# Fifteen more entries in the table that reorders a hybrid attention layer's instruction queues

## The chip, the cores and the metric

The kernel runs on one core of one Trainium2 chip. The metric is the device time of one execution in microseconds (us); "the time" of a kernel is the median of its runs. The core has five engines that this text speaks of: TensorE (PE), VectorE (DVE), ScalarE (ACT), GpSimd (POOL) and SyncE (SP). Each works through its own queue of instructions in order. Here SP does no arithmetic: it issues the kernel's DMA transfers.

## The reference

The program is one layer of a streaming encoder. It takes 1024 prompt rows and 32 sample rows of width 1024, and projects them, after a norm, with one matrix `w_in` to q, k, v and a gate g for two groups of eight heads of 64: group A is band attention (a frame sees its own chunk of 64 and the eight before, with a clipped relative bias), group B is stick-breaking attention. The 32 sample rows also attend to cached keys and values.

```python
def band_attention(q, k, v, q_pos, k_pos, bias_table):
    s = jnp.einsum('bqhd,bkhd->bhqk', q, k).astype(jnp.float32) * ATTN_SCALE
    ...
    w = jax.nn.softmax(s, axis=-1).astype(v.dtype)
    return jnp.einsum('bhqk,bkhd->bqhd', w, v)
def stick_breaking(q, k, v, q_pos, k_pos):
    ...
    after = lax.cumsum(log_1m, axis=3, reverse=True) - log_1m
    w = jnp.where(causal, jnp.exp(log_beta + after), 0.0).astype(v.dtype)
    return jnp.einsum('bhqk,bkhd->bqhd', w, v)
def finish(h, oa, ga, ob, gb, w_out, g_post, p, w_ple, w_ple_gate):
    y = jnp.concatenate([oa * jax.nn.silu(ga), ob * jax.nn.silu(gb)], axis=-1) @ w_out
    h = h + rmsnorm(y, g_post)
    return h + jax.nn.sigmoid(h @ w_ple_gate) * (p @ w_ple)
```

The outputs are both groups of rows and the new k and v of both head groups. All is float32.

## The kernel before

Each float32 operand of a matrix product is split into a high part, a rounded copy, and a low part, the difference (`hnh` and `hnl` for the normed rows, `wh` and `wl` for weights, `kd` and `kl` for keys, `wTh` and `wTl` for attention weights). A product is three matmuls on such parts. ACT mostly casts the high parts; DVE or POOL subtract for the low ones.

The work runs over head pairs 0 to 3 of each group. For a pair of heads the columns of q, k, v are projected (`mm_qA`, `mm_kB` and so on, 352 rows at a time), k and v are turned and stored to the outputs, and then each of the two heads is attended to in eight tiles of 128 rows: scores (`SA`, `SB`), the weights (ACT's exponentials with DVE's minima for A, sigmoids and DVE's scans for B), turned weights, and values (`PVA`, `PVB`). The gates' projections (`mm_gA`, `mm_gB`) come late, then the output projection and what follows it. While attention goes on, the projections of the next pair fill PE's time. The names in the profile count pairs and heads: `swapA31_7` belongs to group A, pair 3, head 1.

Most weights are turned on PE, by `ptwA` and `ptwB`. Tiles 5, 6 and 7 of a group A head, and 4, 5, 6 of group B, take a tour through memory instead (`weights_t`, L1114): DVE turns squares of 32, one DMA stores them in a scratch (`swapA`, 960 KB for A's three tiles), four DMAs load them in another order into `wTl` (240 KB each), ACT casts them to `wTh`, and POOL subtracts in `wTl`. Then PE's `PVA` matmuls can read both.

Two other users of the queue of transfers matter here. The gate matrix and the output matrix get a preparation of their own: quarters `gB` and `oB` of 256 KB are loaded, POOL combines them, and `sum_drg` and `sum_dro` store the results. And the raw columns of `w_in` come as `wr` tiles of 256 KB, two for each projection, which ACT casts.

At the start PE runs twelve `idle` matmuls on zeros, then turns p (`pp`, two parts of 256 KB, to `ptp`), spreads the row `grow` of `g_pre` over all partitions with ones (`gpre`; DVE first casts the row into `wTl` and subtracts), and multiplies p with `w_ple` (`ple`). DVE's norm of x reads `gpre`.

No engine's order is written out by hand. `Recorder` records every operation. `order` (L499) plans from costs and sets the order on each engine. Then `moved` (L576) corrects it by the table `MOVES` (L130): an entry `(engine, i, d)` takes instruction i out of that engine's list and puts it back d places on, or back if d is negative. Entries apply one after the other, so each index counts in the list that those before it have left. Last, `emit` (L616) writes all in the merged order, and the framework adds the semaphore waits. As every operation is written from one line, the profile shows L626 for nearly all of them.

All of SP's transfers go to one DMA queue. Each is given one of eight semaphores in turn, so besides its data an issue waits for the landing of the transfer eight places before it. Whatever is moved in SP's list therefore shifts both the transfers and these waits.

Of the kernel before, what the change touches and what calls it, by code (L numbers as in the profile page):

```python
# [125 lines left out]
def f(ap):  # L126
# [12 lines left out]
    ("DVE", 228, -1), ("ACT", 822, 1), ("SP", 518, 4), ("SP", 532, 9), ("SP", 91, 1),  # L139
    ("SP", 204, 4), ("SP", 115, 10), ("DVE", 492, 7), ("PE", 2963, -10), ("PE", 2964, -10),  # L140
    ("PE", 2965, -10), ("PE", 2966, -10), ("PE", 2967, -10), ("PE", 2968, -10), ("PE", 2969, -10),
    ("PE", 2970, -10), ("PE", 2971, -10),
)


# [1986 lines left out]
```

## Time and profile before

| | |
|---|---|
| time, median of 3 runs | 767.8 us (767.15 to 769.6) |
| the profiled execution's own time | 767.8 us |
| its span, first to last instruction | 766.0 us |
| mean granted TensorE clock | 0.999 |
| busy PE, DVE, ACT, POOL | 757.5, 571.1, 542.2, 509.2 us |
| the one queue of transfers | 164.44 MB, 73.4% of 16 DMA engines' span |

The busy rows are sums over one execution. The chain of waits says which engine ended last at each moment; the waits list says for what an engine stood still, and the timeline shows single instructions with their start, length and the idle time ahead of them. A wait is named by the last of the semaphores to come. SPq in a row is SP's queue issuing a transfer, not the transfer itself.

### The profile page before, as it was taken

To read this page: it belongs to the slowest core of one execution; us is meant where nothing else is said; L and a number is where in the kernel's file an instruction comes from. 1 tells how busy PE (TensorE), PEld (TensorE's weight loads), DVE (VectorE), ACT (ScalarE), POOL (GpSimd) and SP (SyncE) were. 2 spreads that over 40 slices of the span, in tenths; PEclk is the share of its full clock that TensorE was granted. 3 is DMA by queue.
4 is the path that set the end of the run, shared out by engine and by line. 5 is a ranking of instruction groups with operands and counts; after the bars stand their busy time and mean duration, and the time that the engine had idled before them with its cause. 6 is when DMAs were issued, how large, how long until landed. Compare 5 with 4: busy or idle time off the path is not lost.

```text
span 766.0 us, 14225 instructions
## 1 busy us (share of the span) xinstructions
PE 757.5 (99%) x4502; PEld 705.8 (92%) x4502; DVE 571.1 (75%) x1029; ACT 542.2 (71%) x1139; POOL 509.2 (66%) x547
## 2 busy tenths in 40 slices
PE   8999999999999999999999999999999999999997
PEld 7999999999999999999999998999998877888786
DVE  6827567688788778878797577879455787998975
ACT  5647977788688768898897677555438868766461
POOL 5724778996637657669994747788552539697533
PEclk9999999999999999999999999999999999999999
DMA  9646977759776657986859788879578967769644
GB/s 299 219 131 188 243 220 205 219 157 266 183 186 182 148 146 230 214 248 174 212 172 264 173 234 206 240 213 268 167 255 278 319 212 223 260 203 374 218 145 138
DMA packets 198397, 165.35 MB, mean 216 GB/s; under 512 B 65889, under 2 KB 165385, under 8 KB 198322
## 3 DMA queue, kind: packets, MB, share of 16 engines
q1 hardware_dynamic: 198322, 164.44, 73.4%
q8 instruction: 36, 0.59, 0.3%
q14 instruction: 39, 0.32, 0.2%
HBM read 105.72 MB, written 58.91 MB: 215 GB/s over the span
## 4 chain that ended last, share of the span: by engine, by line
PE 92%; ACT 3%; DMA 3%; SPq 1%; DVE 1%; issue 0%; POOL 0%; ACTq 0%; DVEq 0%
PE mm_qA L626 6%; PE mm_kA L626 6%; PE mm_vA L626 6%; PE mm_gB L626 6%; PE mm_gA L626 5%; PE mm_qB L626 5%; PE mm_kB L626 5%; PE mm_vB L626 5%; PE PVB L626 4%; PE SB L626 4%; PE PVA L626 4%; PE SA L626 3%; PE ple L626 3%; PE g1P L626 3%; PE o3P L626 3%; PE o1P L626 3%
## 5 line engine op out<-in xcount | busy, mean ns | idle before, releaser
L626 POOL TENSOR_TENSOR be<-be,om 128x1024 f32<-128x1024 f32 (+8 forms) x66 | 81.8, 1246 | 43.2 <-DVE om L626 13.2
L626 DVE TENSOR_TENSOR_SCAN om<-om,SB 128x384 f32<-128x384 f32 (+5 forms) x96 | 91.6, 965 | 19.3 <-ACT om L626 13.5
L626 POOL TENSOR_TENSOR wTl<-wTl,wTh 128x640 fp32r<-128x640 f32 (+2 forms) x42 | 72.6, 1746 | 15.0 <-ACT wTh L626 11.7
L626 ACT ACTIVATE om<-SB 128x384 f32<-128x384 f32 (+5 forms) x96 | 44.2, 494 | 12.5 <-DVE SB L626 8.4
L626 ACT ACTIVATE be<-SB 128x512 f32<-128x512 f32 (+5 forms) x96 | 45.5, 495 | 9.8 <-PE SB L626 7.4
L626 ACT ACTIVATE be<-be,statA 128x640 f32<-128x640 f32 (+3 forms) x64 | 44.4, 695 | 9.0 <-DVE statA L626 8.8
L626 DVE STREAM_TRANSPOSE om<-be 128x640 f32<-128x640 f32 (+2 forms) x48 | 42.9, 899 | 2.6 <-POOL be L626 1.4
L626 ACT CAST wTh<-wTl 128x640 fp32r<-128x640 f32 (+2 forms) x48 | 35.9, 778 | 11.3 <-DMA wTl<-swapA 7.8
L626 POOL TENSOR_TENSOR oB<-oB,oB 128x256 f32<-128x256 f32 x32 | 26.8, 857 | 13.4 <-DMA oB<-in_w_out_dram 13.4
L626 DVE CUSTOM_DVE_ANT_0 be<-SA,biasA 128x320 f32<-128x320 f32 (+3 forms) x64 | 30.2, 482 | 4.9 <-PE SA L626 3.8
L626 PE MATMUL SB<-kl,LB 128*128 128x384 f32 (+5 forms) x96 | 32.5, 345 | 0.0
L626 PE MATMUL SB<-kdB,LB 128*128 128x384 f32 (+5 forms) x96 | 32.3, 341 | 0.0
L626 POOL TENSOR_TENSOR kl<-stkB,kdB 64x1024 fp32r<-64x1024 f32 x8 | 19.7, 2460 | 18.7 <-ACT kdB L626 17.3
L626 DVE TENSOR_TENSOR wTl<-ptwB,wTh 128x512 fp32r<-128x512 f32 (+3 forms) x48 | 26.1, 547 | 5.7 <-ACT wTh L626 5.1
L626 PE MATMUL SA<-kl,LA 128*128 128x320 f32 (+2 forms) x96 | 30.1, 316 | 0.0
L626 DVE TENSOR_TENSOR SB<-SB,maskb 128x128 f32<-128x128 f32 x64 | 18.0, 293 | 16.0 <-PE SB L626 15.0
L626 PE MATMUL SA<-kdA,LA 128*128 128x320 f32 (+2 forms) x96 | 29.9, 313 | 0.0
L626 ACT CAST wTh<-ptwB 128x512 fp32r<-128x512 f32 (+3 forms) x48 | 22.8, 482 | 9.9 <-PE ptwB L626 9.3
L626 DVE TENSOR_TENSOR wTl<-ptwA,wTh 128x512 fp32r<-128x512 f32 (+3 forms) x48 | 22.5, 480 | 8.9 <-ACT wTh L626 8.1
L626 PE MATMUL PVB<-wTl,v2B 128*128 128x256 f32 (+1 forms) x144 | 24.8, 295 | 0.0
L626 POOL TENSOR_TENSOR gB<-gB,gB 128x256 f32<-128x256 f32 x32 | 24.6, 790 | 0.1
L626 POOL TENSOR_TENSOR h<-h,x 128x512 f32<-128x512 f32 (+1 forms) x18 | 23.8, 1344 | 0.2 <-DVE h L626 0.2
(700 smaller groups left out, 2667.1 us busy)
## 6 DMA issues: line engine op xcount, KB each, us to landing
swapA<-om SPq DMA_DIRECT2D x8, 960.0 KB, 5.7
wTl<-swapA SPq DMA_DIRECT2D x32, 240.0 KB, 5.1
oB<-in_w_out_dram SPq DMA_DIRECT2D x16, 256.0 KB, 3.6
sum_dro<-oB SPq DMA_DIRECT2D x16, 256.0 KB, 4.0
gB<-in_w_ple_gate_dram SPq DMA_DIRECT2D x16, 256.0 KB, 4.3
sum_drg<-gB SPq DMA_DIRECT2D x16, 256.0 KB, 2.5
x<-in_x_prompt_dram SPq DMA_DIRECT2D x16, 256.0 KB, 4.2
h_dr<-h SPq DMA_DIRECT2D x8, 512.0 KB, 3.8
```

Source lines behind the costliest of these rows:

```text
L626: getattr(getattr(tc.nc, o.what[0]), o.what[1])(*args, **kw)
```

## The change

Fifteen entries are added at the end of `MOVES`; nothing else differs. As the table grows by three lines, L626 becomes L629.

```diff
-    ("PE", 2970, -10), ("PE", 2971, -10),
+    ("PE", 2970, -10), ("PE", 2971, -10), ("SP", 2, -1), ("SP", 486, -2), ("SP", 493, -2),
+    ("SP", 494, -2), ("SP", 495, -2), ("SP", 496, -2), ("SP", 197, 6), ("SP", 486, -2),
+    ("SP", 92, -1), ("SP", 330, 4), ("SP", 509, -2), ("SP", 198, 1), ("DVE", 237, -4),
+    ("SP", 445, 6), ("POOL", 335, -1),
```

Thirteen entries are for SP, one is for DVE and one for POOL. They are listed below in the order of the program; one of SP's, (92, -1), exchanges two transfers that read alike. PE's and ACT's orders stay.

1. At the start, p's second part goes ahead of the row of `g_pre`.

SP at the start of the program, before:

```order
L626 DMA pp0_176<-in_p_prompt_dram 128x2x256
L626 DMA grow_171<-in_g_pre_dram 1x1024
L626 DMA pp0_176<-in_p_prompt_dram 128x2x256
L626 DMA wpr0_0True_177<-in_w_ple_dram 128x512
L626 DMA om_179<-in_x_prompt_dram 128x1024
```

And after:

```order
L629 DMA pp0_176<-in_p_prompt_dram 128x2x256 x2
L629 DMA grow_171<-in_g_pre_dram 1x1024
L629 DMA wpr0_0True_177<-in_w_ple_dram 128x512
L629 DMA om_179<-in_x_prompt_dram 128x1024
L629 DMA wpr1_0True_178<-in_w_ple_dram 128x512
```

Both parts of p now stand together, and the row of one partition behind them.

2. In the tour of head 0 of pair 1 (`swapA10_7`), the store of `vtA1` to the output of new A values goes behind six other transfers: the third and fourth load of the tour, a quarter of the output matrix, a load from `cache_a_v` and two stores of new keys.

SP between the first two loads of this tour and the cache load `be`, before (`oB213` is a quarter of the output matrix, `o_dr4` takes a finished piece of head group B, `out_4` is the output of new B keys):

```order
L626 DMA wTl_170<-swapA10_7_123 32x12x160 x2
L626 DMA o_dr4_67<-otB01_0_0_2137 64x256
L626 DMA o_dr4_67<-otB01_0_1_2288 64x256
L626 DMA out_3_dram<-vtA1_1981 128x4x128
L626 DMA wTl_170<-swapA10_7_123 32x12x160
L626 DMA oB213_2557<-in_w_out_dram 128x512
L626 DMA wTl_170<-swapA10_7_123 32x12x160
L626 DMA be_193<-in_cache_a_v_dram 128x4x256
L626 DMA out_4_dram<-ktB1_2441 32x32x32 x2
```

And after:

```order
L629 DMA wTl_170<-swapA10_7_123 32x12x160 x2
L629 DMA o_dr4_67<-otB01_0_0_2137 64x256
L629 DMA o_dr4_67<-otB01_0_1_2288 64x256
L629 DMA wTl_170<-swapA10_7_123 32x12x160 x2
L629 DMA oB213_2557<-in_w_out_dram 128x512
L629 DMA be_193<-in_cache_a_v_dram 128x4x256
L629 DMA out_4_dram<-ktB1_2441 32x32x32 x2
L629 DMA out_3_dram<-vtA1_1981 128x4x128
```

The third and fourth load now stand together, ahead of `oB213`, and the store stands behind all of them.

3. In pair 2's tour of head 0 (`swapA20_7`), the four loads of `wTl` go ahead of a store `sum_drg`. In pair 3's tour of head 0 (`swapA30_7`), the first of the four loads goes behind the stores `swapA3`, `vs_dr` and two of `o_dr`.

4. In the last A tour (`swapA31_7`), the store goes ahead of one load of a `wr_gA` tile, and the four loads go ahead of another and of a `sum_drg` store.

SP around this tour, before (`one_dr3` takes sums of the softmax, `o_dr3` finished pieces of head group A):

```order
L626 DMA wr_gA1_0_5877<-in_w_in_dram 128x4x128
L626 DMA wr_gA1_1_5878<-in_w_in_dram 128x4x128
L626 DMA swapA31_7_144<-om_179 128x1920
L626 DMA o_dr3_66<-otA30_0_0_5887 64x256
L626 DMA o_dr3_66<-otA30_0_1_5888 64x256
L626 DMA wr_gA2_0_5990<-in_w_in_dram 128x4x128
L626 DMA one_dr3_74<-sumA30_3168 16x32
L626 DMA wr_gA2_1_6005<-in_w_in_dram 128x4x128
L626 DMA sum_drg_86<-gB213_5882 128x512
L626 DMA wTl_170<-swapA31_7_144 32x12x160 x4
```

And after:

```order
L629 DMA wr_gA1_1_5878<-in_w_in_dram 128x4x128
L629 DMA swapA31_7_144<-om_179 128x1920
L629 DMA wr_gA1_0_5877<-in_w_in_dram 128x4x128
L629 DMA o_dr3_66<-otA30_0_0_5887 64x256
L629 DMA o_dr3_66<-otA30_0_1_5888 64x256
L629 DMA wr_gA2_0_5990<-in_w_in_dram 128x4x128
L629 DMA one_dr3_74<-sumA30_3168 16x32
L629 DMA wTl_170<-swapA31_7_144 32x12x160 x4
L629 DMA wr_gA2_1_6005<-in_w_in_dram 128x4x128
L629 DMA sum_drg_86<-gB213_5882 128x512
```

The store stands one place earlier and the four loads two; `wr_gA1_0` now follows the store, `wr_gA2_1` and `sum_drg` follow the loads.

5. A load from `cache_b_k` goes ahead of the store of `swapB30_6`. On DVE, the first of two minima of tile 4 of head 1 of pair 1 (`SA11_4`) goes up ahead of four subtractions and sums; on POOL, the subtraction for `wl_vB3_0` goes up ahead of a half of a `gB223` subtraction.

## The prediction, made before the changed kernel ran

> **What bounds the kernel now.** I read the page first: its busy shares, then the chain that ended last, then the waits of TensorE (PE), and then the timeline at each of these waits.
>
> ```profile
> span 766.0 us, 14225 instructions
> PE 757.5 (99%) x4502; PEld 705.8 (92%) x4502; DVE 571.1 (75%) x1029; ACT 542.2 (71%) x1139; POOL 509.2 (66%) x547
> PE 92%; ACT 3%; DMA 3%; SPq 1%; DVE 1%; issue 0%; POOL 0%; ACTq 0%; DVEq 0%
> PE idle L626 <- DVE newh L626: 1.3, 1, 1.3
> PE PVA L626 <- POOL wTl L626: 1.0, 1, 1.0
> PE ptp L626 <- DMA pp<-in_p_prompt_dram: 0.9, 1, 0.9
> PE PVA L626 <- ACT wTh L626: 0.5, 2, 0.4
> ```
>
> PE works 99% of the span, and the chain of waits runs through it for 92%. All its waits together are 1.3 + 1.0 + 0.9 + 0.5 = 3.7 us. The first, 1.3 us before the first instruction, belongs to memsets that the change leaves alone. The change removes no arithmetic and leaves PE's order and ACT's as they were, so as long as TensorE's clock stays as it is, it can win at most the other 2.4 us, a little more where a wait also empties PE's pipeline. The profiled execution took 767.8 us, 1.8 around its span of 766.0; the median is 767.8 as well (767.15 to 769.6), so sums against the one hold for the other. About 0.3%, 2.3 us, is what a measurement of this kernel can tell from no change: the bounds are 765.5 and 770.1.
>
> **The start: p's second part ahead of the row of g_pre.** In these rows a time stands first, then a length; the bracket names the idle time ahead and what ended it.
>
> ```profile
> 1.24 0.35 SPq L626 DMA_DIRECT2D grow<-in_g_pre_dram  x1
> 1.30 2.93 PE L626 MATMUL idle<-newh 128*128 128x256 f32 x12 [1.30 <-DVE newh L626]
> 1.63 0.40 SPq L626 DMA_DIRECT2D pp<-in_p_prompt_dram  x1
> 3.71 0.68 DVE L626 CAST wTl<-grow 1x1024 fp32r<-1x1024 f32 x1 [0.31 <-DMA grow<-in_g_pre_dram]
> 4.42 1.21 DVE L626 TENSOR_TENSOR wTl<-grow,wTl 1x1024 fp32r<-1x1024 f32 x1
> 6.02 1.12 PE L626 MATMUL ptp<-ident,pp 128*128 128x128 f32 x4 [0.93 <-DMA pp<-in_p_prompt_dram]
> 6.79 2.06 PE L626 MATMUL gpre<-wTl,ones 128*128 128x512 f32 x4
> 8.64 2.40 PE L626 MATMUL ple<-wph0True,php 128*128 128x512 f32 x6
> 10.88 0.86 PE L626 MATMUL ple<-wpl0True,php 128*128 128x512 f32 x3
> 11.57 1.56 PE L626 MATMUL ple<-wph1True,php 128*128 128x512 f32 x6
> ```
>
> Moved past one issue, p's second part starts 1.63 - 1.24 = 0.39 us earlier and, if its 4.3 us of flight stay, ends PE's wait by as much: at most 0.4 us is gained. The row of g_pre is issued 0.39 later. Its flight was 1.24 to 3.71, 2.5 us; if that stays, VectorE (DVE) has its CAST and subtraction (0.68 + 1.21) done at 1.63 + 2.47 + 1.92 = 6.0, and the gpre matmuls, from 6.4 on, need the second half of it only at 7.2. But the row now stands behind 256 KB. If it lands no sooner than p, at 5.6, the subtraction ends at 7.5, the third gpre matmul starts 0.3 later than it would, and nearly all is lost again; if p keeps its landing at 5.97, so that the row comes then too, 0.2 us is lost outright. So the ends are a gain of 0.4 and a loss of 0.2. I take a gain of 0.2: p surely moves, and the row's measured 2.5 us is nearer to a small transfer of its own than to p's 4.3.
>
> [...]
>
> **The second A tour of head pair 1 (190 to 205 us).** The 256 KB store of vtA goes behind the fourth wTl load and the load of a w_out quarter, oB. These rows show the loads, oB's reader and PE's reader.
>
> ```profile
> 189.78 0.54 SPq L626 DMA_DIRECT2D out_dram<-vtA  x1
> 191.67 0.59 SPq L626 DMA_DIRECT2D wTl<-swapA  x1
> 196.88 1.43 POOL L626 TENSOR_TENSOR oB<-oB,oB 128x256 f32<-128x256 f32 x2 [1.44 <-DMA oB<-in_w_out_dram]
> 198.55 1.98 ACT L626 CAST wTh<-wTl 128x640 fp32r<-128x640 f32 x3 [2.55 <-DMA wTl<-swapA]
> 199.35 5.26 POOL L626 TENSOR_TENSOR wTl<-wTl,wTh 128x640 fp32r<-128x640 f32 x3 [1.04 <-ACT wTh L626]
> 200.58 1.50 PE L626 MATMUL PVA<-wTh,v2A 128*128 128x512 f32 x8 [0.17 <-ACT wTh L626]
> 204.75 1.24 PE L626 MATMUL PVA<-wTl,v2A 128*128 128x128 f32 x6
> ```
>
> The fourth load is issued a good half microsecond earlier and no longer has the store ahead of it, so ScalarE's (ACT's) casts come earlier and PE's 0.17 at 200.58 (0.3 by the distance of matmul starts) goes. Yet GpSimd (POOL) does its three subtractions in 5.26, ends at 204.61, and PE's next reader starts at 204.75: only 0.14 of slack. And POOL's own subtraction of oB, 1.43, stands ahead of them in its queue: oB now comes behind a 240 KB load, so POOL starts it later. What is won at 200.58 is then given back at 204.75. Ends: a gain of 0.3, and a loss of 0.5 if oB's lateness passes whole into POOL's chain. I take 0, as the slack of 0.14 says.
>
> **The last A tour (445 to 467 us).** Here is the larger term. The store swapA31_7 goes ahead of one of two wr_gA loads, and its four loads go ahead of another wr_gA and of a sum_drg store. The three rows with KB have the median time from issue to landing last; the last two, for stretches of 2 us, end with the granted clock, the DMA engines' busy share and GB/s.
>
> ```profile
> 445.70 0.46 SPq L626 DMA_DIRECT2D swapA<-om  x1
> 450.93 0.38 SPq L626 DMA_DIRECT2D wr_gA<-in_w_in_dram  x1
> 451.94 2.69 SPq L626 DMA_DIRECT2D wTl<-swapA  x4
> 460.82 1.36 ACT L626 CAST wTh<-wTl 128x640 fp32r<-128x640 f32 x2 [3.91 <-DMA wTl<-swapA]
> 461.62 4.60 POOL L626 TENSOR_TENSOR wTl<-wTl,wTh 128x640 fp32r<-128x640 f32 x3 [3.11 <-DMA oggA<-o_dr]
> 463.33 1.50 PE L626 MATMUL PVA<-wTh,v2A 128*128 128x512 f32 x8 [0.37 <-ACT wTh L626]
> 466.27 1.32 PE L626 MATMUL PVA<-wTl,v2A 128*128 128x128 f32 x6 [1.00 <-POOL wTl L626]
> wr_gA<-in_w_in_dram SPq DMA_DIRECT2D x5, 256.0 KB, 3.3
> sum_drg<-gB SPq DMA_DIRECT2D x1, 256.0 KB, 3.9
> wTl<-swapA SPq DMA_DIRECT2D x4, 240.0 KB, 5.5
> 450.00:452.00 2.00, 2.00 (x16) 1.98 (x15) 0.49 (x2) 1.98 (x5) 0.72 (x3) 1.00 0.66 189
> 454.00:456.00 2.00, 2.00 (x14) 2.00 (x13) 1.94 (x3) 1.95 (x6) 0.00 (x0) 1.00 1.06 275
> ```
>
> Two transfers of 256 KB stand ahead of the four loads. At 275 GB/s, the rate while the queue is full, 512 KB take 1.9 us; at 189 GB/s 2.8. The loads can be issued one after the other only once the store has landed; that comes sooner too, with 256 KB less ahead of it. So the loads end, and ACT's casts start, about 2.2 us earlier: 458.6. ACT stood idle for 3.91 there, from 456.9, and POOL for 3.11, from 458.5, so both can follow. The casts (with the third, until 463.27) then end near 461.1, and PE asks for them at 463.33 - 0.37 = 462.96. The subtractions, 461.62 + 4.60 = 466.22, end near 464.0; PE asks for them at 466.27 - 1.00 - 0.37 = 464.9. Both waits go: 1.37 by the rows, 1.7 with the pipeline refilled. The margin is 0.9; the earlier landing must be at least 1.3 for all of it, and one of 0.7 still brings half.
>
> The delayed transfers: wr_gA1_0 stays ahead of the loads and only swaps with the store (its reader, a cast of ACT, is at 455.77); wr_gA2_1 is read from 480 on and has 20 us; nothing near reads sum_drg.
>
> Then I asked what is late next. SP, which issues the transfers, is busy from 467 to 490, and one chain there leads from it to PE.
>
> ```profile
> 484.55 0.58 SPq L626 DMA_DIRECT2D og_dr<-sggA  x1
> 486.84 0.46 ACT L626 ACTIVATE sggA<-mm_gA 128x352 f32<-128x352 f32 x1 [2.62 <-DMA og_dr<-sggA]
> 489.14 0.52 DVE L626 TENSOR_TENSOR sggA<-mm_gA,sggA 128x352 f32<-128x352 f32 x1
> 490.17 0.32 PE L626 MATMUL mm_gA<-hnh,wh_gA 128*128 128x352 f32 x1
> ```
>
> ACT waits for the og_dr store to free its buffer, DVE follows, and PE takes the freed bank at 490.17, 0.51 after DVE's end at 489.66. A PE that runs 1.37 early meets this chain unless og_dr is early too. If nothing of SP's work moves, 0.5 is kept; if all does, 1.4 to 1.7. SP's queue is tied to landings, and those gain the room that the share of 0.66 leaves, so I take 1.1.
>
> **The other moves**, each at 0. Four loads of A2's tour ahead of a sum_drg store, and A3's first load behind four small stores: no wait of PE stands there among the 3.7 us, so PE's 99% covers both. The cache_b_k load ahead of a store, one maximum of DVE a few places up, one subtraction of POOL up: the readers are not waited for by PE. Uncovered, each costs one issue or operation, 0.4 to 1.4 us, on a queue that is 66 to 75% busy.
>
> **The sum.** 0.2 + 0 + 1.1 + 0 = 1.3 us: 767.8 - 1.3 = 766.5. The ends are 0.4 + 0.3 + 1.7 = 2.4 gained (765.4) and 0.2 + 0.5 lost against 0.5 gained, 0.2 lost (768.0).
>
> **The rivals.**
>
> *Given back at 490* (0.2). For it: 0.51 of slack only, and SP issues without a pause. Against it: the transfers have gained room. The A3 term is then 0.5: 767.8 - 0.7 = 767.1.
>
> *A later clock at the start* (0.08, the slower side). The page shows the granted clock as full, yet from 6.79 to 8.64 four 512-column matmuls take 0.46 each, and from 10.88 to 11.57 three take 0.23: the full rate comes near 10.4, 4.4 us after PE's wait ended at 6.02. The 2.9 us of the twelve idle matmuls had not brought it. So a busy stretch of 2.9 to 4.4 us seems to be needed. If the row of g_pre lands after about 5.7, PE gets a second gap, before the third gpre matmul, inside the stretch that ended at 10.4. If stretches are fixed, the full rate then comes a whole one later, and 2.9 to 4.4 us at half rate lose 1.5 to 2.2. With 1.8 of that, 0.2 lost to the gap and 1.1 gained later: 768.7. For it speaks that the row now stands behind 256 KB; against it, the 0.3 by which it may come late is short beside a stretch.
>
> *An earlier clock* (0.17). If a wait of 0.5 in place of 0.9 lets the stretch before count as busy, the full rate comes 2.9 to 4.4 us sooner, at 6.0 to 7.5, and about nine matmuls save 0.2 each, 1.8. The first norm tiles, which come by DMA, may take a part of it back; I keep 0.6 to 1.8, and with 1.1 that is 764.9 to 766.1, in the middle 765.5. Against it: 0.5 of idle time is still there.
>
> [...]
>
> *The change does not do what it says*: the four loads land no earlier because the store's landing sets them. Then 767.6. It is inside the range, and I count it with the forecast.
>
> **How the numbers follow.** The forecast has 0.55, the rivals 0.2, 0.08 and 0.17. The likeliest is 766.5. The range leaves out the better half of the earlier clock and the worse half of the later one: 765.0 to 768.5. Faster by over 0.3% is over half of the earlier clock and the top of the forecast: 0.16. Slower by over 0.3%, past 770.1, needs the later clock and the oB chain together: 0.04. The rest, 0.80, is within 0.3%.
>
> **What the profile after would show.** Right: PE's waits for POOL wTl and ACT wTh are gone from its list; ACT's cast near 458.6 (counted from before's clock); PE's first ptp wait near 0.5; the matmul after the 490 chain with a wait of 0 to 0.9. Wrong: the casts still at 460 or later; a PE wait at gpre; the change of matmul spacing from 0.46 to 0.23 away from 10.4; a new wait for POOL wTl near 204.

## The result, and the profile after

The changed kernel took 765.99 us (median of ten runs, 764.83 to 767.04) beside 768.69 us of the kernel before (ten runs, 767.07 to 770.88): a ratio of 0.9964 with a 95% interval of 0.9952 to 0.9977, or 2.7 us (1.8 to 3.7) faster. In a second series it was 765.86 beside 767.32, a ratio of 0.9976 (0.9961 to 0.9990), or 1.8 us. The forecast was 1.3 us.

The page of the profiled execution after, which took 765.79 us: its span, the busy times, the chain, and then PE's list of waits.

```profile
span 764.0 us, 14232 instructions
PE 755.8 (99%) x4502; PEld 703.7 (92%) x4502; DVE 571.2 (75%) x1029; ACT 543.7 (71%) x1139; POOL 507.2 (66%) x547
PE 94%; DMA 4%; ACT 1%; DVE 1%; SPq 1%; issue 0%; ACTq 0%; DVEq 0%
PE idle L629 <- DVE newh L629: 1.3, 1, 1.3
PE ple L629 <- ACT wph1True L629: 1.0, 1, 1.0
PE PVA L629 <- DVE v2A L629: 0.5, 1, 0.5
PE gpre L629 <- DVE wTl L629: 0.5, 1, 0.5
```

PE is as full as before and loses 3.3 us to waits in place of 3.7. The three waits that could be won are gone; three others have come, for a cast at the start (1.0), for v2A at 429 us and for the row of g_pre (0.5 each).

PE's order is the same in both kernels, so the start of one and the same matmul can be compared. The first pair of rows is the first transposition of a normed x tile; then come the ends of a stretch around the tour of pair 1, and of a stretch around the last tour. Before:

```profile
13.67 0.60 PE L626 MATMUL ptx<-ident,be 128*128 128x128 f32 x4
199.37 0.30 PE L626 MATMUL SA<-kdA,LA 128*128 128x320 f32 x1
206.26 0.27 PE L626 MATMUL ptxsA<-ident,be 128*32 128x128 f32 x1
457.84 0.39 PE L626 MATMUL SB<-kdB,LB 128*128 128x512 f32 x1
467.43 0.34 PE L626 MATMUL SB<-kdB,LB 128*128 128x384 f32 x1
```

The same five after:

```profile
12.36 0.60 PE L629 MATMUL ptx<-ident,be 128*128 128x128 f32 x4
198.07 0.30 PE L629 MATMUL SA<-kdA,LA 128*128 128x320 f32 x1
204.49 0.27 PE L629 MATMUL ptxsA<-ident,be 128*32 128x128 f32 x1
457.20 0.39 PE L629 MATMUL SB<-kdB,LB 128*128 128x512 f32 x1
464.90 0.34 PE L629 MATMUL SB<-kdB,LB 128*128 128x384 f32 x1
```

So in these two profiles PE is 1.31 us ahead after the start, 1.30 ahead of the tour of pair 1 and 1.77 behind it (0.47 won there), only 0.64 at 457 (1.13 lost on the way), and 2.53 behind the last tour: 1.89 won there. At the end 2.0 is left, the difference of the spans.

The start after. The bracket names the idle time and what ended it.

```profile
4.03 1.21 PE L629 MATMUL ptp<-ident,pp 128*128 128x128 f32 x8
4.33 0.68 DVE L629 CAST wTl<-grow 1x1024 fp32r<-1x1024 f32 x1 [0.93 <-DMA grow<-in_g_pre_dram]
6.32 0.73 PE L629 MATMUL gpre<-wTl,ones 128*128 128x512 f32 x2 [0.45 <-DVE wTl L629]
6.88 1.57 PE L629 MATMUL ple<-wph0True,php 128*128 128x512 f32 x6
8.46 1.06 ACT L629 ACTIVATE be<-om 128x1024 f32<-128x1024 f32 x1 [1.64 <-DMA om<-in_x_prompt_dram]
10.17 1.66 PE L629 MATMUL ple<-wph1True,php 128*128 128x512 f32 x6 [1.01 <-ACT wph1True L629]
```

All eight ptp matmuls run in one piece: no wait for p is left. The row of g_pre is cast 0.62 later than before, and PE waits 0.45 for it, the second gap that the prediction named. The six ple matmuls take 1.57 us, where they took 2.40; below, "half rate" and "full rate" mean this distance between matmuls, since the granted clock is listed as 1.00 in both profiles from 2 to 12 us. Then, at 10.17, PE waits for a cast of ACT that stands behind ACT's work on the first x tile, which came by DMA only at 8.46.

The last tour after:

```profile
449.41 2.62 SPq L629 DMA_DIRECT2D wTl<-swapA  x4
457.93 1.36 ACT L629 CAST wTh<-wTl 128x640 fp32r<-128x640 f32 x2 [1.65 <-DMA wTl<-swapA]
458.74 4.62 POOL L629 TENSOR_TENSOR wTl<-wTl,wTh 128x640 fp32r<-128x640 f32 x3 [0.85 <-ACT wTh L629]
462.16 1.39 PE L629 MATMUL PVA<-wTh,v2A 128*128 128x512 f32 x8
463.83 1.23 PE L629 MATMUL PVA<-wTl,v2A 128*128 128x128 f32 x6
```

Neither PVA row has a bracket any more. Counted from PE's own row at 457.20 the casts start at +0.73; before it was 460.82 - 457.84 = +2.98, so they are 2.25 us earlier.

### The profile page after: what moved, and what is told of

It is laid out like the page before. It is cut to its first block, busy times and chain, and to the rows that moved or that the text cites. A ratio compares the mean times of both kernels' runs of the same rounds, so it can differ in the third digit from the quotient of the medians.

```text
span 764.0 us, 14232 instructions
## 1 busy us (share of the span) xinstructions
PE 755.8 (99%) x4502; PEld 703.7 (92%) x4502; DVE 571.2 (75%) x1029; ACT 543.7 (71%) x1139; POOL 507.2 (66%) x547
## 4 chain that ended last, share of the span: by engine, by line
PE 94%; DMA 4%; ACT 1%; DVE 1%; SPq 1%; issue 0%; ACTq 0%; DVEq 0%
PE mm_qA L629 6%; PE mm_kA L629 6%; PE mm_vA L629 6%; PE mm_gB L629 6%; PE mm_vB L629 6%; PE mm_gA L629 6%; PE mm_kB L629 6%; PE PVB L629 5%; PE SB L629 4%; PE PVA L629 4%; PE mm_qB L629 4%; PE SA L629 3%; PE ple L629 3%; PE g1P L629 3%; PE o3P L629 3%; PE o1P L629 3%
## 5 line engine op out<-in xcount | busy, mean ns | idle before, releaser
L629 POOL TENSOR_TENSOR be<-be,om 128x1024 f32<-128x1024 f32 (+8 forms) x66 | 81.4, 1240 | 43.8 <-DVE om L629 14.5
L629 DVE TENSOR_TENSOR_SCAN om<-om,SB 128x384 f32<-128x384 f32 (+5 forms) x96 | 91.5, 965 | 17.8 <-ACT om L629 12.4
L629 POOL TENSOR_TENSOR wTl<-wTl,wTh 128x640 fp32r<-128x640 f32 (+2 forms) x42 | 72.3, 1739 | 12.5 <-ACT wTh L629 8.3
L629 ACT ACTIVATE om<-SB 128x384 f32<-128x384 f32 (+5 forms) x96 | 44.4, 493 | 11.8 <-DVE SB L629 7.7
L629 ACT ACTIVATE be<-SB 128x512 f32<-128x512 f32 (+5 forms) x96 | 45.5, 495 | 9.5 <-PE SB L629 7.4
L629 ACT ACTIVATE be<-be,statA 128x640 f32<-128x640 f32 (+3 forms) x64 | 44.4, 695 | 8.8 <-DVE statA L629 8.6
L629 DVE STREAM_TRANSPOSE om<-be 128x640 f32<-128x640 f32 (+2 forms) x48 | 42.9, 899 | 2.6 <-POOL be L629 1.4
L629 ACT CAST wTh<-wTl 128x640 fp32r<-128x640 f32 (+2 forms) x48 | 36.0, 779 | 9.1 <-DMA wTl<-swapA 4.9
L629 POOL TENSOR_TENSOR oB<-oB,oB 128x256 f32<-128x256 f32 x32 | 26.3, 841 | 13.3 <-DMA oB<-in_w_out_dram 13.2
L629 DVE CUSTOM_DVE_ANT_0 be<-SA,biasA 128x320 f32<-128x320 f32 (+3 forms) x64 | 30.2, 481 | 5.3 <-PE SA L629 3.8
L629 PE MATMUL SB<-kl,LB 128*128 128x384 f32 (+5 forms) x96 | 32.5, 345 | 0.0
L629 PE MATMUL SB<-kdB,LB 128*128 128x384 f32 (+5 forms) x96 | 32.3, 341 | 0.0
L629 POOL TENSOR_TENSOR kl<-stkB,kdB 64x1024 fp32r<-64x1024 f32 x8 | 19.7, 2460 | 18.4 <-ACT kdB L629 18.3
L629 PE MATMUL SA<-kl,LA 128*128 128x320 f32 (+2 forms) x96 | 30.1, 315 | 0.0
L629 DVE TENSOR_TENSOR SB<-SB,maskb 128x128 f32<-128x128 f32 x64 | 17.9, 293 | 16.0 <-PE SB L629 15.2
L629 PE MATMUL SA<-kdA,LA 128*128 128x320 f32 (+2 forms) x96 | 29.9, 313 | 0.0
L629 DVE TENSOR_TENSOR wTl<-ptwB,wTh 128x512 fp32r<-128x512 f32 (+3 forms) x48 | 26.1, 546 | 4.9 <-ACT wTh L629 4.2
L629 ACT CAST wTh<-ptwB 128x512 fp32r<-128x512 f32 (+3 forms) x48 | 22.8, 482 | 9.4 <-PE ptwB L629 8.9
L629 DVE TENSOR_TENSOR wTl<-ptwA,wTh 128x512 fp32r<-128x512 f32 (+3 forms) x48 | 22.5, 480 | 8.8 <-ACT wTh L629 7.9
L629 PE MATMUL PVB<-wTl,v2B 128*128 128x256 f32 (+1 forms) x144 | 24.9, 295 | 0.0
L629 POOL TENSOR_TENSOR gB<-gB,gB 128x256 f32<-128x256 f32 x32 | 24.2, 773 | 0.8 <-DMA gB<-in_w_ple_gate_dram 0.7
L629 POOL TENSOR_TENSOR h<-h,x 128x512 f32<-128x512 f32 (+1 forms) x18 | 23.8, 1348 | 0.2 <-DVE h L629 0.2
```

Source lines behind the costliest of these rows:

```text
L629: getattr(getattr(tc.nc, o.what[0]), o.what[1])(*args, **kw)
```

## The experiments

Each kernel is the one before with some of the entries, unless something else is said, and each was profiled once. Its time stands beside that of the kernel before in the same series; the difference in us is worked out from the ratio, and the difference of the two medians can be another. "The tour's stretch" is the time between the two SB rows shown above, 9.59 before and 7.70 after.

### The start

Only the first entry:

```diff
-    ("PE", 2970, -10), ("PE", 2971, -10),
+    ("PE", 2970, -10), ("PE", 2971, -10), ("SP", 2, -1),
```

> Only p's second part goes ahead of the row of g_pre; the other fourteen entries are left out. In the changed kernel's trace this place is worth 1.3 us (the ptx matmuls start at 12.36 instead of 13.67), because PE's wait for p is gone and the matmul spacing falls to 0.23 us near 4.4 us instead of near 10.4. Theory 'adds up': the places add, so the time is 1.3 us under the kernel before (ratio 0.9983). Rival 'held later': transfers that keep their own time cap PE's lead at about 0.6 us at the A values of pair 3 (430 us) and take the rest at the last A tour, where PE then waits the longer, so the time is 0 to 0.4 us under before. Second rival, of the clock: the early doubling was the luck of one execution; then the spacing changes anywhere between 4 and 14 us here.

Measured: 767.37 beside 768.25, a ratio of 0.9996 (0.9985 to 1.0006): 0.3 us faster, between 1.2 faster and 0.5 slower. Its profile has the x tile and the first ptx here:

```profile
7.47 1.06 ACT L627 ACTIVATE be<-om 128x1024 f32<-128x1024 f32 x1 [0.28 <-DMA om<-in_x_prompt_dram]
11.38 0.60 PE L627 MATMUL ptx<-ident,be 128*128 128x128 f32 x4
```

PE is even 2.29 us ahead at ptx in this execution, and the time says 0.3, not to be told from none; the 1.3 of "adds up" lies outside the interval. Of the 2.29 only 0.33 is left at the SB row of the last tour (457.51 beside 457.84); 0.7 of it went to a wait for v2A at 429 us, as "held later" has it. So the place in one profile does not tell what the entry is worth.

All entries but that one:

```diff
-    ("PE", 2970, -10), ("PE", 2971, -10),
+    ("PE", 2970, -10), ("PE", 2971, -10), ("SP", 486, -2), ("SP", 493, -2),
...
```

> All entries but the one at the start. 'Adds up': 2.0 - 1.3 = 0.7 us under before (ratio 0.9991). 'Held later': the lead of 0.46 us from pair 1's tour passes the places at 325 and 430 us, where the changed kernel lost 0.4 and 0.75 us of its lead, without loss, and the last A tour brings PE to the same place as in the changed kernel, so 1.7 to 2.2 us under before (ratio 0.9975), as much as the changed kernel within its interval.

Measured: 766.75 beside 768.25, 0.9982 (0.9972 to 0.9993), 1.4 us faster. Between the two expectations; they aren't told apart by the time. The profile tells more, since its start is that of the kernel before:

```profile
5.47 1.12 PE L627 MATMUL ptp<-ident,pp 128*128 128x128 f32 x4 [0.39 <-DMA pp<-in_p_prompt_dram]
9.14 1.06 ACT L627 ACTIVATE be<-om 128x1024 f32<-128x1024 f32 x1 [1.92 <-DMA om<-in_x_prompt_dram]
13.05 0.60 PE L627 MATMUL ptx<-ident,be 128*128 128x128 f32 x4
205.48 0.85 PE L627 MATMUL PVA<-wTl,v2A 128*128 128x128 f32 x4 [0.26 <-POOL wTl L627]
```

With the old order of the start, p came at 5.47 here and not at 6.02, and ptx was 0.62 ahead of the first profile. (The last row belongs to pair 1's tour, below.) The start rows of ten profiles, the kernels with the entry first:

| kernel | six ple matmuls take | ACT starts the x tile | ptx | from one to the other |
|---|---|---|---|---|
| after | 1.57 | 8.46 | 12.36 | 3.90 |
| after, again | 1.57 | 8.37 | 12.58 | 4.21 |
| only the first entry | 1.55 | 7.47 | 11.38 | 3.91 |
| without two entries | 1.56 | 8.62 | 12.79 | 4.17 |
| without the last tour's | 1.56 | 8.81 | 12.72 | 3.91 |
| before | 2.40 | 7.92 | 13.67 | 5.75 |
| all but the first entry | 1.55 | 9.14 | 13.05 | 3.91 |
| only the last tour's | 1.58 | 7.49 | 11.68 | 4.19 |
| only its loads | 1.71 | 8.57 | 12.65 | 4.08 |
| only its store | 1.71 | 8.17 | 12.08 | 3.91 |

In nine of these ten, with and without the entry, ptx follows the x tile by 3.9 to 4.2 us: ACT works on the x tile, then casts `wph1`, and PE's ple matmuls of 10.17 in the profile after read that cast. In the four rows with 4.08 to 4.21 the cast began 0.2 to 0.3 us later still, right after the landing of the quarter of `w_ple` that it reads. So these transfers end the start, and p does not. The first profile of before is the odd one: its matmuls ran at half rate until 10.4, and ptx was late by itself. In the mean of the five rows each ptx is at 12.37 with the entry and at 12.63 without, 0.26 apart, in a scatter of 2 us.

Then the opposite move, p's second part behind 768 KB:

```diff
-    ("PE", 2970, -10), ("PE", 2971, -10),
+    ("PE", 2970, -10), ("PE", 2971, -10), ("SP", 2, 2),
```

> The opposite of the change's first entry, alone: p's second part goes behind the first quarter of w_ple and the first tile of x, 768 KB, so it should land some 2 us later, near 7.5 to 8, and PE's gap ahead of the second ptp grows to about 3 us. If the start is sensitive to p (an idle gap of this size keeps the matmul spacing at 0.46 until 10 to 12 us in every execution), the time is 1 to 2 us over the kernel before (ratio 1.0013 to 1.0026). If the landing of the first x tile and the norm behind it set the end of the start anyway, x lands no later here, and the time is within 0.5 us of before.

Measured: 770.98 beside 767.67, 1.0039 (1.0022 to 1.0055), 3.0 us slower, more than expected.

```profile
8.17 1.12 PE L627 MATMUL ptp<-ident,pp 128*128 128x128 f32 x4 [3.09 <-DMA pp<-in_p_prompt_dram]
8.94 2.06 PE L627 MATMUL gpre<-wTl,ones 128*128 128x512 f32 x4
10.80 2.76 PE L627 MATMUL ple<-wph0True,php 128*128 128x512 f32 x6
```

The gap is 3.09, and the half rate (six ple in 2.76) lasts beyond 12. So the start is sensitive to p on the late side: p has some slack in the order before, but not the 2 to 3 us by which it came later here. In this profile, with its gap of 3.09, the full rate came late as well.

Last, the gap was covered without moving a transfer: the twelve idle matmuls got 384 columns in place of 256, in the kernel before and in the changed one.

```diff
-        nc.tensor.matmul(idle[:, 0:256], newest[0][:, 0:P], newest[0][:, P:P + 256], start=True, stop=True)
+        nc.tensor.matmul(idle[:, 0:384], newest[0][:, 0:P], newest[0], start=True, stop=True)
```

> The kernel before with wider idle matmuls at the start (384 columns in place of 256), so that PE is busy until about 5.1 us and the gap ahead of p's second part, which landed at 4.85 to 5.97 in six profiles, is covered or short. No transfer moves. If the upper half of before's runs (768 to 771) comes from executions whose matmul spacing halves only near 10.4 us because of that gap, the median falls by 0.3 to 1.0 us, the upper quartile by 1 or more, and the spacing halves before 8.2 in the profile. If the first x tile sets the end of the start in nearly all executions, the time is as before within 0.3, as PE has a wait of 0.7 to 1.7 us there that takes up the longer idle matmuls.

> The changed kernel with the same wider idle matmuls. Its second part of p lands at 4.2 to 5.0, so hardly a gap is left to cover: the same as the changed kernel within 0.3, about 1.9 us under before. If PE's clock is still late in some of its executions, 0.2 to 0.6 less than that.

Measured: 767.15 beside 768.11, 0.9988 (0.9975 to 1.0000), 0.9 us faster in the kernel before; 765.18, 0.9966 (0.9945 to 0.9987), 2.6 us faster in the changed one, from seven runs, which is not to be told from the changed kernel's own 0.9964 and 0.9976. The first, in its profile:

```profile
1.30 4.21 PE L626 MATMUL idle<-newh 128*128 128x384 f32 x12 [1.30 <-DVE newh L626]
6.44 0.66 PE L626 MATMUL ptp<-ident,pp 128*128 128x128 f32 x4 [0.43 <-DMA pp<-in_p_prompt_dram]
8.67 1.06 ACT L626 ACTIVATE be<-om 128x1024 f32<-128x1024 f32 x1 [0.49 <-DMA om<-in_x_prompt_dram]
12.62 0.60 PE L626 MATMUL ptx<-ident,be 128*128 128x128 f32 x4
```

Here p landed late, as in the first profile, and yet the second half of ptp took 0.66 (1.12 before) and ptx followed the x tile by 3.95. That speaks for the gap as the cause of the late full rate, and for a gain from closing it in some executions of the kernel before; it is one profile. The interval only just reaches zero, so the time alone does not show it. In the series of the first four experiments 19 of 35 runs of before were above 768 us and 2 of 11 with the first entry alone; with the wider idle matmuls it was 2 of 11, beside 9 of 17. That hints that the entry and the idle matmuls trim the slow executions; it does not show it, since all but the first entry, a faster kernel by 1.4, had none of 12 there either.

### The last A tour

Only its six entries:

```diff
-    ("PE", 2970, -10), ("PE", 2971, -10),
+    ("PE", 2970, -10), ("PE", 2971, -10), ("SP", 486, -2), ("SP", 493, -2),
+    ("SP", 494, -2), ("SP", 495, -2), ("SP", 496, -2), ("SP", 486, -2),
```

> Only the moves of the last A tour (its store ahead of one wr_gA load, its four loads ahead of another and of the sum_drg store). 'Adds up', and the prediction's own term of 1.1: both waits at 463 and 466 us go, 1.4 to 1.7 us, and 0.3 to 0.5 is given back at 490, so 1.0 to 1.4 us under before (ratio 0.9985). 'Held later': PE reaches the tour without any lead, and the loads still set the time, so as much as the whole change, 2.0. If the tour is worth nothing alone, the time is as before.

Measured: 766.25 beside 768.25, 0.9986 (0.9974 to 0.9998): 1.1 us by the ratio, 2.0 by the medians. The tour's stretch is 463.79 - 456.10 = 7.69:

```profile
456.10 0.39 PE L627 MATMUL SB<-kdB,LB 128*128 128x512 f32 x1
463.79 0.34 PE L627 MATMUL SB<-kdB,LB 128*128 128x384 f32 x1
```

All but these six:

```diff
-    ("PE", 2970, -10), ("PE", 2971, -10),
+    ("PE", 2970, -10), ("PE", 2971, -10), ("SP", 2, -1), ("SP", 197, 6), ("SP", 198, 1),
+    ("SP", 92, -1), ("SP", 330, 4), ("SP", 509, -2), ("DVE", 237, -4),
+    ("SP", 445, 6), ("POOL", 335, -1),
```

> All entries but those of the last A tour. In five profiles of kernels with these entries PE gained 1.7 to 1.9 us from 463 to 468 us, so without them the two waits there must be back, about as long as PE's lead makes them, and of the 2.7 us of the whole change at most 1 is left: 0.3 to 1.0 us under before. If the other entries carry the change, 2.0 under.

Measured: 766.99 beside 767.67, 0.9995 (0.9983 to 1.0008): 0.4 us faster, not to be told from none. POOL's wait is back:

```profile
464.83 1.32 PE L627 MATMUL PVA<-wTl,v2A 128*128 128x128 f32 x6 [0.90 <-POOL wTl L627]
```

Then the tour's two parts apart. Only the four loads:

```diff
-    ("PE", 2970, -10), ("PE", 2971, -10),
+    ("PE", 2970, -10), ("PE", 2971, -10), ("SP", 493, -2),
+    ("SP", 494, -2), ("SP", 495, -2), ("SP", 496, -2),
```

> Of the last A tour only the four loads move, ahead of a wr_gA load and the sum_drg store (512 KB); the store stays. The prediction has 1.9 to 2.8 us of earlier landing from these 512 KB, against 1.3 needed, so both waits go, and PE gains 1.4 to 1.9 us between 463 and 468. If the landing of the store sets the loads, PE gains there less than 0.5.

```profile
457.46 0.39 PE L627 MATMUL SB<-kdB,LB 128*128 128x512 f32 x1
458.56 1.36 ACT L627 CAST wTh<-wTl 128x640 fp32r<-128x640 f32 x2 [2.02 <-DMA wTl<-swapA]
465.19 0.34 PE L627 MATMUL SB<-kdB,LB 128*128 128x384 f32 x1
```

Measured: 766.23 beside 767.67, 0.9985 (0.9973 to 0.9998), 1.2 us faster. The casts start at +1.10 from PE's row, 1.9 earlier than before, and the stretch is 7.73: nearly all is won.

Only the store:

```diff
-    ("PE", 2970, -10), ("PE", 2971, -10),
+    ("PE", 2970, -10), ("PE", 2971, -10), ("SP", 486, -2), ("SP", 486, -2),
```

> Of the last A tour only the store moves, ahead of one wr_gA load (256 KB); the loads stay behind the other wr_gA load and sum_drg. By the prediction the earlier landing of the store brings 0.7 to 0.9 us if the loads follow it, so about half of both waits goes, 0.5 to 0.9 us between 463 and 468. If the 512 KB ahead of the loads set them, nothing changes there, since those transfers only take the room; if the store's landing sets all, both waits go.

```profile
455.74 0.39 PE L627 MATMUL SB<-kdB,LB 128*128 128x512 f32 x1
458.40 1.36 ACT L627 CAST wTh<-wTl 128x640 fp32r<-128x640 f32 x2 [3.59 <-DMA wTl<-swapA]
463.86 1.31 PE L627 MATMUL PVA<-wTl,v2A 128*128 128x128 f32 x6 [1.00 <-POOL wTl L627]
465.01 0.34 PE L627 MATMUL SB<-kdB,LB 128*128 128x384 f32 x1
```

Measured: 767.57 beside 767.67, 1.0001 (0.9989 to 1.0012). The casts start at +2.66, and the stretch is 9.27. In the five other kernels whose loads stood as before the casts start at +2.24 to +2.98, 2.53 in the mean, so nothing of the earlier store shows in them. The 512 KB ahead of the loads set their landing: without them the casts start at +1.10, and while they stood there the earlier store was worth nothing (1.0001). Once the loads have moved as well, it does bring the casts forward: they start at -0.25 to +0.73 in the six kernels with both moves, beside +1.10 with the loads alone. PE gains no more from that, as its waits are gone already.

Over all thirteen profiles (the ten of the table, p behind 768 KB, and the two with wider idle matmuls) the stretch is 7.69 to 7.73 in the seven kernels whose loads were moved, and 8.87 to 9.59 in the six others (9.17 in the mean; the first profile of before is the longest).

### The two moves for pairs 2 and 3, and the whole change again

All entries but `("SP", 330, 4)` and `("SP", 445, 6)`:

```diff
-    ("PE", 2970, -10), ("PE", 2971, -10),
+    ("PE", 2970, -10), ("PE", 2971, -10), ("SP", 2, -1), ("SP", 486, -2), ("SP", 493, -2),
...
```

> All entries but two: the four loads of pair 2's tour stay behind the sum_drg store, and the first load of pair 3's first tour stays ahead of the four small stores. If these two moves cost the 0.37 us at 325 us and the 0.75 us at 430 us, the time is 3.1 us under before, 1.1 under the changed kernel. If the losses come from transfers that keep their own time whatever these two moves do, the lead at 430 us is again near 0.6 and the time that of the changed kernel within 0.3.

Measured: 765.88 beside 768.25, 0.9977 (0.9963 to 0.9990), 1.8 us: like the changed kernel. Between the 206 and the 457 us rows PE takes 252.5 us here, 252.7 in the profile after and 251.6 before. So these two entries are neither the cause of that loss nor worth anything that the time shows.

The changed kernel once more:

> The changed kernel itself once more, beside the next two. So far the whole change gave 2.7 us (interval 1.8 to 3.7), its parts alone 0.3 (start), 1.1 (last A tour) and 0.4 (all but the last tour). If the parts simply add, 1.5 to 1.9 us under before here (ratio about 0.998); if they help each other, 2.7 again (0.9965). The start: PE's place at 55 us is again given by the landing of the first x tile, 9.7 us minus that landing ahead of the profile of before.

Measured: 1.8 us, as said above; the parts (0.3, 1.1 to 1.2, and 0.4 with the first among it) add up to 1.5 or so. Whether the whole is worth 1.8 or 2.7 is open within the intervals. Its profile has a wait that no other had:

```profile
366.78 1.16 PE L629 MATMUL PVB<-wTh,v2B 128*128 128x256 f32 x8 [1.19 <-DVE v2B L629]
```

Such a wait for a v tile (v2A at 429 in the first profile after, v2B here) takes 0.5 to 1.2 us of PE's lead in one execution and none in another of the same kernel. Another wait of this kind stands at 510 us, 0.8 for `Vl2sB` of DVE, in four of the thirteen profiles (the last tour's entries alone, p behind 768 KB, and both with wider idle matmuls). There PE takes 1.0 us longer from 490 to 512 us; neither profile of the changed kernel has it.

## Why the prediction came out as it did

The direction and the range (765.0 to 768.5) held; the forecast of 1.3 us is half of the 2.7 first measured and three quarters of the 1.8 of the second series. The chance of 0.80 for "within 0.3%" stands beside a measured 0.36% and, repeated, 0.24%: on the bound. Two of its own signs of being wrong came: a PE wait at gpre, and the change of the matmul spacing away from 10.4. Both belong to the start, and neither cost anything that the time shows.

*The last tour* was forecast by the right mechanism: casts 2.2 us earlier, measured 2.25 (and 1.9 from the loads alone), counted from the first profile of before; both waits gone, 1.4 to 1.7 expected, 1.89 measured between the two profiles. The step that was mis-sized is "I take 1.1", with up to 0.9 given back to the og_dr chain at 490. The place is real. In the profile after:

```profile
482.48 0.39 PE L629 MATMUL SB<-kdB,LB 128*128 128x512 f32 x1
487.31 0.52 DVE L629 TENSOR_TENSOR sggA<-mm_gA,sggA 128x352 f32<-128x352 f32 x1
487.88 0.43 PE L629 MATMUL mm_gA<-hnh,wh_gA 128*128 128x352 f32 x1
```

From SB to this matmul it is 5.40, where before it was 490.17 - 485.01 = 5.16, so 0.24 is given back there. But in five of the seven kernels with moved loads it is 5.16 again, and nothing is given back at this place: in those five the og_dr store is issued 0.5 to 1.2 us ahead of the SB row, in the other two up to 0.1 behind it. What makes SP earlier there was not tested. The rival "given back at 490" needed all of SP's work to stand still. On the other side the first profile of before was the worst of six for this tour (9.59 against a mean of 9.17), so the entries are worth about 1.5 at this place in the mean and not 1.9. Timed alone all six gave 1.1 and the loads 1.2; that the first is just the forecast is in part luck, since its interval reaches from 0.2 to 2.0 and the discount for 490 found no ground in most traces.

The prediction also let the loads follow an earlier store. With the store moved alone the casts start within the scatter of the kernels whose loads stood as before, and the time stays: that part of the step is not borne out.

*Pair 1's tour* was taken as 0, because of POOL's slack of 0.14 at 204.75. It brought 0.47 between the two profiles.

```profile
195.43 1.98 ACT L629 CAST wTh<-wTl 128x640 fp32r<-128x640 f32 x3 [0.74 <-DMA wTl<-swapA]
195.90 1.44 POOL L629 TENSOR_TENSOR oB<-oB,oB 128x256 f32<-128x256 f32 x2 [1.76 <-DMA oB<-in_w_out_dram]
197.29 4.80 POOL L629 TENSOR_TENSOR wTl<-wTl,wTh 128x640 fp32r<-128x640 f32 x3
203.01 1.21 PE L629 MATMUL PVA<-wTl,v2A 128*128 128x128 f32 x6
```

The casts came 3.1 us earlier in time, 1.8 of it beyond PE's lead, and POOL went from oB straight to its three subtractions, which end at 202.09, 0.9 ahead of PE. The fear that oB would be late was right by 0.3 only. The step that failed is that all is given back at 204.75: before, POOL had stood idle for 1.04 between oB and the subtractions, until ACT's casts came, and oB's lateness went into that room. The subtractions themselves also took 4.80 in place of 5.26; they stand back to back in both traces, and why they were faster is not shown. In one kernel of six with these entries POOL was late after all (0.26, the row at 205.48). And in three of the seven kernels without them PE crossed this place in 6.43 to 6.49 us too, beside 6.89 in the first profile of before, so in the mean the entries earn about 0.3 here. By the SB row at 457 nothing of that is left: from 199.37 on, PE takes 259.1 us in the mean of the six kernels with them and 258.9 in the seven without.

*The start* was forecast at 0.2 and measured alone at 0.3, in an interval that holds zero, but by a wrong step: "at most 0.4 us is gained" by p's earlier landing, read from a profile in which the full rate was late. Usually the start ends with the first x tile plus 3.9 to 4.2 us, and PE mostly has a wait ahead of that, 1.0 us in the profile after, in which p's landing is hidden; where the full rate is late, as in the first profile of before (half rate until 10.4, ptx 5.75 behind the x tile), there was more for the entry to win. That is the rival of an earlier clock, priced at 0.6 to 1.8 and seen at 1.31 in the two profiles; but the early full rate came in kernels without the entry as well. Where the full rate comes differs between executions of one kernel: in the first profile of the changed kernel the ptp matmuls come closer together from 4.4 us on, 3.1 us after PE's first matmul, and all eight take 1.21 us; in the second they keep the half rate to the end, and the full rate comes after 6.1 us, 4.8 after the first matmul. Neither lists a wait of PE in between, so the busy stretch of 2.9 to 4.4 us, an estimate of the prediction from one trace, is not one fixed length:

```profile
4.03 1.91 PE L629 MATMUL ptp<-ident,pp 128*128 128x128 f32 x8
```

Of the five profiled kernels with the old start and the narrow idle matmuls, four had the six ple matmuls in 1.55 to 1.71 us and one in 2.40; their gaps ahead of p differ too (none listed, 0.16, 0.20, 0.39, and 0.93 in the slow one), so these do not show whether the gap or something else sets the point.

The later clock, the slower side, was not seen with the change. The gap for the row of g_pre came, at 0.45, but not because the row was late: DVE had its subtraction done at 6.26, near the 6.0 that the prediction has. PE was early, as at the full rate it stood ready for the third gpre matmul at 5.87 and not at 7.2. (By the single matmuls in the trace of before, that figure should be 7.4: the third gpre matmul starts at 7.79 there.)

*The other moves* were put at 0, and the time bears it out as far as it was tried: with the two moves of pairs 2 and 3 left out it is the same. The cache_b_k load, DVE's and POOL's moves were not tried one by one. (What the prediction calls a maximum of DVE is a minimum.)

*The waits that come in their place* were looked for at one point, 490, and were found in others: at 10.17, 429 and 366, and in other kernels at 510. PE's lead of 1.77 shrank to 0.64 between 206 and 457 in the first profile after. Which of these transfers is late in which execution stays open.

## What to carry to other kernels

One profile of a kernel that is busy 99% gives the size of a wait to about its own scatter: the same tour took 8.87 to 9.59 us in six kernels whose loads stood as before, and the start 3.9 to 4.2 or 5.75 behind the first x tile. Look at two or three executions before you price a wait of a microsecond, and time the part alone. A load that many things wait for goes ahead of transfers that nobody needs soon (1.2 us for the four loads alone); moving the store that feeds it was worth nothing here (1.0001) as long as those still stood between.

## What the runs showed of the hardware

A longer run of idle matmuls (the first ptp matmul at 5.31 us in place of 4.04) cost PE nothing that the time shows (767.15 beside 768.11), and the second half of ptp ran at full rate (0.66 us, 1.12 before) even with p at 6.44. And a change of 0.4 us in an issue moved a landing by more: p's second part landed at 4.85 to 6.40 us in six profiles with the old order and at 4.20 to 5.02 in six with the new one, 1.1 us earlier in the mean. With the old order it ended a wait of PE at 5.09 to 6.44 in five of six profiles with the usual start, while with the new order all eight ptp matmuls followed one another without a listed wait in six of six.
